# Down projection of a hybrid decoder layer: weight combinations moved to DVE, and the next pair of weight blocks emitted in two portions within the current pair

## The chip, the cores and the metric

One NeuronCore of a Trainium2 chip. A core has five engines with an instruction queue each: TensorE (PE in the profile, its weight loads PEld), VectorE (DVE), ScalarE (ACT), GpSimd (POOL) and SyncE (SP), which here only issues DMAs. Each queue is worked off in order; engines wait for each other by semaphores. The metric is the device time of one execution in microseconds; before the change the median of three runs is 1985.99 us (1985.06 to 1986.43).

## The reference

The kernel computes one layer of a hybrid decoder: a norm, one wide projection, four branches (gated recurrence, pooling, stick-breaking attention, short convolution), an output projection, and then an MLP with squared ReLU, for 1024 tokens and 1024 channels in float32. The change touches only the last product, `act` (1024 tokens x 4096) by `w_down` (4096 x 1024):

```python
    h2 = rmsnorm(x, norm2_g)
    act = jnp.square(jax.nn.relu(jnp.einsum('bld,df->blf', h2, w_up)))
    return x + jnp.einsum('blf,fd->bld', act, w_down)
...
    return rmsnorm(h[:, FRONT:], final_norm_g)
```

## The kernel before

All big products run on TensorE with float32 operands that are split into a high and a low part (`split`, lines 77 and 78: ACT casts the high part, DVE subtracts it from the source to get the low part). A product of two such operands is three matmuls: high by high, high by low, low by high.

**The down projection** takes the 4096 rows of `w_down` in 32 blocks of 128. The first four are multiplied plainly (line 1017 adds their products to `x1`, which is shown as `x`). The other 28 go through a Strassen scheme: two blocks of rows and the two halves of 512 columns make a 2 x 2 arrangement, whose product takes seven multiplications in place of eight, of combinations of the weight quarters and of the activations. The combinations of the activations were already formed in the up projection and lie in `sum_dram`. Those of the weights are formed by `down_w(u)` for u = 0 to 13.

`down_w(u)` loads two row blocks `w1` and `w2` (lines 1037 and 1038, tiles `raw`, two buffers in all, so one u at a time; for u = 1 tiles `lo`), forms four subtractions of 128x512 on POOL (lines 1046, 1048, 1049 and 1053, the first two into a tile `hi`), and splits five pieces into `h` and `l` (three of 512 columns, two of 1024). One call thus is 2 DMAs, 4 subtractions, 5 casts on ACT and 5 subtractions on DVE. The results lie in tiles `wb` or `wa`, by turns from pair to pair, four buffers of each name: two calls fill one name.

A **pair** `c` (0 to 6) uses the weights of u = 2c and 2c + 1, accumulated in PSUM. It has four **units** `m` (0 to 3), each for token blocks `m` and `m + 4`. A unit loads its activation combinations (`down_s`, line 1059, into `s_raw`, which has one buffer), splits them (`s_hi` by ACT, its low part in `wide` by DVE; then the remaining two blocks, named `s_late` or `lo` by turns) and does seven products of six matmuls each: 42 matmuls of 128x512, line 1081. The methods `one`, `two`, `three` and `four` of `Unit` hold the products; `two` and `four` of a unit are emitted after `one` and `three` of the next one. After each product DVE adds the bank to `x1` (lines 1088, 1092, 1096, 1100 and 1104) or writes the sum into the bank of product two (line 1086, tile `tr`), and one is copied by ACT (line 1098). A bank that DVE has yet to read is not written again, so the next product in the same bank waits for it: product six of a unit for line 1086.

**What sets the order.** The code is emitted as it stands in the loop over `c` and `m` at the end; a scheduler then fixes the order on each engine when the program is built, with emission order as priority, and hoists what is ready by its own estimate. Tiles come from rotating buffers: a tile's first write waits until the readers of its buffer's last use are done. In the loop before, both calls of `down_w` for a pair stand ahead of its four units:

```python
        for c in range(NU // 2):
            tw = [down_w(2 * c), down_w(2 * c + 1)]
...
            for m in range(4):
                unit = Unit(tw, c, m)
```

Of the kernel before, what the change touches and what calls it, by code (L numbers as in the profile page):

```python
# [47 lines left out]
def hybrid_trunk_kernel(ctx: ExitStack, tc: tile.TileContext, x_tok, metas, vecs, gains, w_in, w_br, w_pool,  # L48
                        w_o, w_up, w_dn, lvl_mask, out):
    nc = tc.nc  # L50
# [19 lines left out]
    def new(pl, shape, dt, tag, bufs=None):  # L70
        return pl.tile(shape, dt, tag=tag, name=nm(tag), **({} if bufs is None else {"bufs": bufs}))

    def split(hi, lo, src, eng=None, heng=None):
        if heng:
            heng.tensor_copy(hi, src)
        else:
            nc.scalar.copy(hi, src)  # L77
        (eng or nc.vector).tensor_sub(lo, src, hi.bitcast(F32))  # L78
# [118 lines left out]
    with ExitStack() as st:  # L197
# [192 lines left out]
        for i, (c0, n) in enumerate(FCH):  # L390
            last = i == len(FCH) - 1
# [524 lines left out]
    with ExitStack() as st:  # L916
# [12 lines left out]
        def pair_of(pl, tags, bufs, shape):  # L929
            return tuple(new(pl, shape, F32R, tag, bufs) for tag in tags)  # L930
# [102 lines left out]
        def down_w(u):  # L1033
            h, l = pair_of(dw, (("wb", "wb"), ("wa", "wa"))[u // 2 % 2], 4, [P, 7 * 512])
            f = FS + 2 * u
            w1, w2 = (new(wst, [P, D], F32, "lo" if u == 1 else "raw") for _ in range(2))
            nc.sync.dma_start(w1, w_dn[f])
            nc.sync.dma_start(w2, w_dn[f + 1])
            b11, b12, b21, b22 = w1[:, :512], w1[:, 512:], w2[:, :512], w2[:, 512:]
            ta = new(wst, [P, D], F32, "hi")  # L1040

            def put(c0, src):
                sl = (slice(None), slice(c0, c0 + src.shape[1]))
                split(h[sl], l[sl], src)

            nc.gpsimd.tensor_sub(ta[:, :512], b12, b11)
            put(0, b11)
            nc.gpsimd.tensor_sub(ta[:, 512:], b22, ta[:, :512])
            nc.gpsimd.tensor_sub(b12, b22, b12)
            put(512, w2)  # L1050
            put(1536, ta)
            put(2560, b12)
            nc.gpsimd.tensor_sub(b21, b21, ta[:, 512:])
            put(3072, b21)
            return h, l

# [80 lines left out]
        def final(b, eh):  # L1137
            es, fs = slice(eh * 512, (eh + 1) * 512), slice((1 - eh) * 512, (2 - eh) * 512)
            o = outs.pop()
            bias = new(small, [P, 1], F32, "bias")  # L1140
            nc.vector.tensor_scalar(bias, sum_sq(x1[:, b, fs], o[:, fs]), 4.0 / D, 4.0 * EPS, op0=ALU.mult, op1=ALU.add)
            nc.gpsimd.tensor_mul(x1[:, b, fs], x1[:, b, fs], fg[:, fs])
            y = rstd_of(sum_sq(x1[:, b, es], o[:, es]), D, bias)
            nc.scalar.mul(o[:, fs], x1[:, b, fs], y)
            nc.scalar.dma_start(out[b, :, fs], o[:, fs])
            nc.vector.scalar_tensor_tensor(o[:, es], x1[:, b, es], y, fg[:, es], op0=ALU.mult, op1=ALU.mult)
            nc.sync.dma_start(out[b, :, es], o[:, es])

        prev, last = None, NU // 2 - 1
        for c in range(NU // 2):  # L1150
            tw = [down_w(2 * c), down_w(2 * c + 1)]
            if c == last:
                fg = new(wst, [P, D], F32, "hi")
                nc.sync.dma_start(fg, gains[2])
                wide = [new(dw, [P, 7 * 512], F32, ("wa", "wb")[c % 2]) for _ in range(3)]
                outs = [t[:, i * D:(i + 1) * D] for t in wide for i in range(3)]
            for m in range(4):
                unit = Unit(tw, c, m)
                if c == last and m == 3:
                    unit.end(prev)  # L1160
                    break
                unit.one()
                if prev:
                    prev.two()
                unit.three()
                if c == last:
                    final(m, 1)
                if prev:
                    prev.four()
                    if c == last and m:  # L1170
                        final(prev.m + 4, 0)
                prev = unit


def _level_masks():
# [57 lines left out]
```

## Time and profile before

| | |
|---|---|
| median of three runs | 1985.99 us |
| profiled execution | 1990.17 us |
| its span in the profile | 1988.4 us |
| last matmul to the end of the span | about 8 us |
| down projection with Strassen, first line 1086 to the last matmul | 1698 to 1980 us |

The profile is of one execution. Its page begins with the busy time of each engine; a view by stretches gives the same for chosen windows, with the granted TensorE clock (1.00 is full speed), the mean share of the 16 DMA engines and the rate. A view of waits lists, for an engine, what it stood still for: total, number, longest. In a timeline row stand the start, the duration, the engine, the line, the operation, the output and input tiles, and in brackets the idle time just before it and what ended it. Starts in a full DVE queue lie closer together than the durations, since an instruction begins while the one ahead still drains. How the engines shared the last stretch of the stage:

```profile
1830.00:1880.00 50.00, 49.00 (x216) 40.27 (x215) 42.83 (x55) 20.56 (x27) 12.45 (x9) 1.00 0.42 149
1930.00:1988.00 58.00, 47.14 (x204) 38.07 (x204) 46.05 (x92) 28.70 (x62) 10.67 (x8) 0.97 0.34 120
```

After the bounds and the length of a window come the busy times of PE, PEld, DVE, ACT and POOL, each with its number of instructions.

### The profile page before, as it was taken

How to read it: one execution, taken by the hardware profiler on the slowest of the kernel's cores; microseconds unless marked ns; L12 is line 12 of the kernel's file. 1: busy time of each engine (PE TensorE's matmuls, PEld its weight loads, DVE VectorE, ACT ScalarE, POOL GpSimd, SP SyncE). 2: the span in 40 equal slices, each digit the busy share in tenths (PEclk: the TensorE clock that was granted, in tenths of full speed). 3: DMA queues.
4: the chain of work that ended last, by engine and by line, in shares of the span. 5: the costliest groups of instructions: out<-in, count | busy, mean ns of one | idle time of the engine just before them, and what ended most of it. 6: DMA issues, size and time to landing. Idle time of an engine off the chain costs nothing.

```text
span 1988.4 us, 25775 instructions
## 1 busy us (share of the span) xinstructions
PE 1934.6 (97%) x9974; PEld 1650.6 (83%) x9974; DVE 1294.7 (65%) x1783; ACT 844.2 (42%) x1452; POOL 329.9 (17%) x280
## 2 busy tenths in 40 slices
PE   9999999999998999999999999999999999999998
PEld 8889899988898888888887888788888887777876
DVE  6677877666767754344334567479555547888887
ACT  6556654233323433343333112255544544343435
POOL 1000001111100033333320000000323212222322
PEclk9999999999999999999999999999999999999999
DMA  3100111110102233333326554242454557343433
GB/s 130 42 33 22 42 34 49 54 43 33 33 32 80 74 151 125 148 107 128 118 105 235 187 187 161 79 147 88 140 170 138 154 164 256 127 143 140 152 131 137
DMA packets 112076, 224.61 MB, mean 113 GB/s; under 512 B 8129, under 2 KB 58817, under 8 KB 111954
## 3 DMA queue, kind: packets, MB, share of 16 engines
q1 hardware_dynamic: 56706, 175.22, 25.8%
q10 hardware_dynamic: 55248, 47.75, 7.1%
q8 instruction: 78, 1.28, 0.3%
q14 instruction: 44, 0.36, 0.1%
HBM read 157.40 MB, written 65.54 MB: 112 GB/s over the span
## 4 chain that ended last, share of the span: by engine, by line
PE 73%; DVE 11%; issue 9%; DMA 4%; ACT 3%; POOL 1%; POOLq 0%; ACTq 0%; DVEq 0%; SPq 0%
PE mm L704 18%; PE mm L104 9%; PE mm L103 9%; PE mm L102 9%; PE z L704 9%; PE tr L704 5%; PE mm L1081 2%; DMA s_raw<-sum_dram 2%; PE av L351 1%; PE z L571 1%; DVE wb L78 1%; DMA raw<-in_w_dn_dram 1%; DVE wa L78 1%; PE z L1081 1%; DVE keep L328 1%
## 5 line engine op out<-in xcount | busy, mean ns | idle before, releaser
L102 PE MATMUL mm<-h_hi,hi 128*128 128x384 f32 (+4 forms) x880 | 304.7, 347 | 0.4 <-ACT h_hi L77 0.4
L104 PE MATMUL mm<-h_hi,lo 128*128 128x384 f32 (+4 forms) x880 | 297.3, 338 | 5.8 <-DVE lo L78 5.8
L103 PE MATMUL mm<-h_lo,hi 128*128 128x384 f32 (+4 forms) x880 | 297.0, 338 | 0.5 <-DVE h_lo L78 0.4
L104 PEld LDWEIGHTS mm<-h_hi,lo 128*128 128x128 f32 x880 | 167.5, 190 | 14.2 <-DVE lo L78 6.2
L103 PEld LDWEIGHTS mm<-h_lo,hi 128*128 128x128 f32 x880 | 168.1, 191 | 7.2 <-DVE h_lo L78 1.3
L102 PEld LDWEIGHTS mm<-h_hi,hi 128*128 128x128 f32 x880 | 167.2, 190 | 6.9 <-ACT h_hi L77 0.9
L681 POOL TENSOR_TENSOR sf<-raw 128x512 f32<-128x512 f32 x30 | 40.9, 1363 | 772.0 <-DMA raw<-in_w_up_dram 448.8
L78 DVE TENSOR_TENSOR sl<-sf,sh 128x1024 fp32r<-128x1024 f32 x68 | 83.3, 1225 | 127.6 <-ACT sh L77 127.6
L78 DVE TENSOR_TENSOR lo<-raw,hi 128x1024 fp32r<-128x1024 f32 x76 | 96.3, 1267 | 52.6 <-ACT hi L77 52.4
L77 ACT CAST hi<-raw 128x1024 fp32r<-128x1024 f32 x76 | 79.9, 1053 | 79.7 <-PE mm L103 43.4
L704 PE MATMUL mm<-th,sh 128*128 128x512 f32 x272 | 105.9, 389 | 0.0
L704 PE MATMUL mm<-tl,sh 128*128 128x512 f32 x272 | 105.8, 389 | 0.0
L704 PE MATMUL mm<-th,sl 128*128 128x512 f32 x272 | 105.8, 389 | 0.0
L328 DVE TENSOR_TENSOR_SCAN keep<-keep 128x1040 f32<-128x1040 f32 (+3 forms) x64 | 88.9, 1389 | 25.7 <-ACT keep L321 18.9
L77 ACT CAST sh<-sf 128x1024 fp32r<-128x1024 f32 x68 | 71.5, 1052 | 80.2 <-PE z L704 41.7
L102 PE MATMUL mm<-b_hi,eh 128*128 128x512 f32 x256 | 99.6, 390 | 1.6 <-DVE mixed L873 1.6
L103 PE MATMUL mm<-b_lo,eh 128*128 128x512 f32 x256 | 100.1, 391 | 0.1
L104 PE MATMUL mm<-b_hi,el 128*128 128x512 f32 x256 | 99.6, 390 | 0.5 <-DVE el L78 0.5
L78 DVE TENSOR_TENSOR el<-raw,eh 128x512 fp32r<-128x512 f32 x34 | 36.6, 1076 | 61.8 <-ACT eh L77 61.8
L323 POOL TENSOR_SCALAR_AFFINE_SELECT keep<-keep 128x128 f32<-128x128 f32 x64 | 22.4, 350 | 302.2 <-ACT keep L321 262.1
L77 ACT CAST s_hi<-s_raw 128x1280 fp32r<-128x1280 f32 x28 | 35.4, 1265 | 85.2 <-DMA s_raw<-sum_dram 78.7
L77 ACT CAST at_h<-tr 128x384 fp32r<-128x384 f32 (+2 forms) x112 | 54.6, 496 | 36.5 <-PE tr L338 34.9
(439 smaller groups left out, 5019.8 us busy)
## 6 DMA issues: line engine op xcount, KB each, us to landing
raw<-in_w_in_dram SPq DMA_DIRECT2D x76, 512.0 KB, 3.6
s_raw<-sum_dram SPq DMA_DIRECT2D x28, 896.0 KB, 4.8
gate_dram<-go ACTq DMA_DIRECT2D x32, 512.0 KB, 2.6
go<-gate_dram SPq DMA_DIRECT2D x32, 512.0 KB, 3.9
raw<-in_w_up_dram SPq DMA_DIRECT2D x32, 512.0 KB, 3.7
raw<-in_w_dn_dram SPq DMA_DIRECT2D x29, 512.0 KB, 4.8
sum_dram<-go ACTq DMA_DIRECT2D x52, 256.0 KB, 4.6
sum_dram<-sums ACTq DMA_DIRECT2D x39, 256.0 KB, 4.6
```

What stands on the lines that cost most here:

```text
L77: nc.scalar.copy(hi, src)
L78: (eng or nc.vector).tensor_sub(lo, src, hi.bitcast(F32))
L102: nc.tensor.matmul(ps, lh, rh, start=first, stop=False)
L103: nc.tensor.matmul(ps, lh, rl, start=False, stop=False)
L104: nc.tensor.matmul(ps, ll, rh, start=False, stop=last)
L323: nc.gpsimd.affine_select(out=t[:, :P], in_=t[:, :P], compare_op=ALU.is_gt, fill=1.0, base=0, pattern=[[1, P]], channel_multiplier=-1)
L328: nc.vector.tensor_tensor_scan(t, t, t, 1.0, op0=ALU.mult, op1=ALU.min)
L351: nc.tensor.matmul(av[:, :w], pair.vv[e][:, b, :], a[:, b, :w], start=i == 0 and a is at[0], stop=i == len(order) - 1 and a is at[1])
L571: nc.tensor.matmul(ps[:, c * 64:(c + 1) * 64], xc, low, start=True, stop=True)
L681: eng.tensor_add(s12[:, 0], a21, a22)
L704: nc.tensor.matmul(ps, lhs[i][x][:, k, :], rhs[i][y][:, k, :], start=fresh and k == 0 and n == 0, stop=k == 3 and n == 2, skip_group_check ...
L1081: nc.tensor.matmul(ps, x, y[:, rs], start=fresh and k == 0 and n == 0, stop=k == 1 and n == 2, skip_group_check=not fresh)
```

## The change

The four subtractions of `down_w` are issued on DVE instead of POOL. And the two calls for the next pair are made inside the current pair: the first behind unit 1, the second behind unit 2; the two of pair 0 stay ahead of the loop. Lines behind the inserted one move by one to three.

```diff
-            nc.gpsimd.tensor_sub(ta[:, :512], b12, b11)
+            nc.vector.tensor_sub(ta[:, :512], b12, b11)
             put(0, b11)
-            nc.gpsimd.tensor_sub(ta[:, 512:], b22, ta[:, :512])
-            nc.gpsimd.tensor_sub(b12, b22, b12)
+            nc.vector.tensor_sub(ta[:, 512:], b22, ta[:, :512])
+            nc.vector.tensor_sub(b12, b22, b12)
             put(512, w2)
             put(1536, ta)
             put(2560, b12)
-            nc.gpsimd.tensor_sub(b21, b21, ta[:, 512:])
+            nc.vector.tensor_sub(b21, b21, ta[:, 512:])
             put(3072, b21)
             return h, l
...
         prev, last = None, NU // 2 - 1
+        coming = [down_w(0), down_w(1)]
         for c in range(NU // 2):
-            tw = [down_w(2 * c), down_w(2 * c + 1)]
+            tw, coming = coming, []
...
                     if c == last and m:
                         final(prev.m + 4, 0)
                 prev = unit
+                if c < last and m in (1, 2):
+                    coming.append(down_w(2 * c + 1 + m))
```

Three places show how the order moves. All are in pair 1; numbers behind a name tell buffers apart and differ between the two programs.

DVE, from the middle of unit 2 to the `wide` of unit 3. Before the change (`mm_14655`, `z_14656` and `tr_14657` are unit 2, `mm_14594` unit 1, `wide_14710` unit 3, `wb_14790` the second block of pair 2):

```order
L1086 TENSOR_TENSOR tr_14657<-mm_14655,x_2171_13933 128x512
L78 TENSOR_TENSOR wb_14790<-raw_14791,wb_14789 128x512
L1088 TENSOR_TENSOR x_2171_13933<-z_14656,x_2171_13933 128x512
L1092 TENSOR_TENSOR x_2171_13933<-mm_14594,x_2171_13933 128x512
L1096 TENSOR_TENSOR x_2171_13933<-mm_14655,x_2171_13933 128x512
L78 TENSOR_TENSOR wide_14710<-s_raw_14707,s_hi_14709 128x1280
```

With the change (`mm_14676` and `z_14677` are unit 2, `mm_14594` unit 1, `wide_14752` unit 3, `wb_14729` the second block of pair 2):

```order
L1096 TENSOR_TENSOR x_2171_13933<-mm_14676,x_2171_13933 128x512
L78 TENSOR_TENSOR wb_14729<-raw_14730,wb_14728 128x512
L1048 TENSOR_TENSOR hi_14734<-raw_14731,hi_14734 128x512
L1049 TENSOR_TENSOR raw_14730<-raw_14731,raw_14730 128x512
L1100 TENSOR_TENSOR x_2171_13933<-z_14677,x_2171_13933 128x512
L78 TENSOR_TENSOR wb_14729<-raw_14731,wb_14728 128x1024
L1104 TENSOR_TENSOR x_2171_13933<-mm_14594,x_2171_13933 128x512
L78 TENSOR_TENSOR wb_14729<-hi_14734,wb_14728 128x1024
L78 TENSOR_TENSOR wb_14729<-raw_14730,wb_14728 128x512
L1053 TENSOR_TENSOR raw_14731<-raw_14731,hi_14734 128x512
L78 TENSOR_TENSOR wide_14752<-s_raw_14749,s_hi_14751 128x1280
```

The second block's subtractions and splits now stand within unit 2, and unit 3's `wide` has moved behind lines 1100 and 1104. From the `wide` of unit 2 to that of unit 3 there are now 14 instructions of 128x512 and two of 128x1024 between them; before there were nine of 128x512. In pairs 2 to 5 this stretch reads the same with the change. The other stretches from one `wide` to the next have, with the change, six instructions of 128x512 (unit 0 to 1), eleven of 128x512 and two of 128x1024 (unit 1 to 2), and eleven of 128x512 (unit 3 to the next pair's unit 0).

TensorE, where it turns from unit 2 to unit 3. Before, with the last matmuls of unit 1's fourth product ahead:

```order
L1081 MATMUL mm_14594<-wa_14503,lo_14591 128x512
L1081 MATMUL mm_14716<-wa_14482,s_hi_14709 128x512
L1081 MATMUL mm_14716<-wa_14483,s_hi_14709 128x512
L1081 MATMUL mm_14716<-wa_14482,wide_14710 128x512
L1081 MATMUL mm_14716<-wa_14503,s_hi_14709 128x512
```

With the change; the last matmul of unit 1's fourth product, which releases line 1104 above, stands ahead of these, with four other rows between:

```order
L1081 MATMUL mm_14676<-wa_14443,s_late_14673 128x512
L1081 MATMUL mm_14758<-wa_14360,s_hi_14751 128x512
L1081 MATMUL mm_14758<-wa_14361,s_hi_14751 128x512
L1081 MATMUL z_14759<-wa_14360,s_hi_14751 128x512
L1081 MATMUL z_14759<-wa_14361,s_hi_14751 128x512
L1081 MATMUL mm_14676<-wa_14442,s_late_14673 128x512
L1081 MATMUL mm_14758<-wa_14360,wide_14752 128x512
```

Between the end of that fourth product and the first matmul that needs `wide` stand ten matmuls now, and two before: unit 2's late product and unit 3's high parts have been drawn in between. From the first matmul with one unit's `wide` to that of the next it is 38, 46, 42 and 42 matmuls with the change (unit 0 to 1, 1 to 2, 2 to 3, 3 to the next pair's unit 0), and 42 each before.

SP, the loads in pair 1 from unit 2 on, as a piece of the difference:

```order
-L1059 DMA s_raw_14646<-sum_dram 128x2x896
-L1037 DMA raw_14791<-in_w_dn_dram 128x1024
-L1059 DMA s_raw_14707<-sum_dram 128x2x896
-L1038 DMA raw_14792<-in_w_dn_dram 128x1024
+L1059 DMA s_raw_14667<-sum_dram 128x2x896
+L1037 DMA raw_14730<-in_w_dn_dram 128x1024
+L1038 DMA raw_14731<-in_w_dn_dram 128x1024
+L1059 DMA s_raw_14749<-sum_dram 128x2x896
+L1037 DMA raw_14934<-in_w_dn_dram 128x1024
+L1038 DMA raw_14935<-in_w_dn_dram 128x1024
 L1059 DMA s_raw_14810<-sum_dram 128x2x896
```

Both loads of the second block for pair 2 now stand ahead of unit 3's activations, and the first block for pair 3 is loaded ahead of pair 2's first unit instead of behind it. Each load of `raw` waits on SP's queue for its buffer, and the load of `s_raw` behind it with it.

## Prediction

> **What bounds the kernel now.** I read the page first, then the stretches of the down projection, then who makes TensorE wait there, then DVE and POOL around one such wait.
>
> ```profile
> PE 1934.6 (97%) x9974; PEld 1650.6 (83%) x9974; DVE 1294.7 (65%) x1783; ACT 844.2 (42%) x1452; POOL 329.9 (17%) x280
> core 0: us, PE busy (x) PEld busy (x) DVE busy (x) ACT busy (x) POOL busy (x), PEclk, DMA share, GB/s
> 1680.00:1730.00 50.00, 45.40 (x193) 35.37 (x192) 47.51 (x56) 20.12 (x26) 20.99 (x15) 1.00 0.39 127
> 1730.00:1780.00 50.00, 49.77 (x219) 40.63 (x218) 39.71 (x52) 18.78 (x25) 13.60 (x9) 1.00 0.42 143
> 1780.00:1830.00 50.00, 46.63 (x197) 37.47 (x196) 40.45 (x50) 22.11 (x30) 13.08 (x9) 0.97 0.39 135
> 1880.00:1930.00 50.00, 47.98 (x210) 38.88 (x208) 43.28 (x51) 21.16 (x30) 18.32 (x12) 1.00 0.44 151
> PE mm L1081 <- DVE tr L1086: 9.2, 7, 2.6
> PE mm L1081 <- DVE wide L78: 2.2, 3, 1.2
> ```
>
> TensorE is busy 97% of the span, and in this stage too it is the bound, less a few waits: the first stretch loses 4.6 us, the second 0.2. The second stretch gives its pace: 49.77 us over 219 matmuls, 0.227 us each, so a unit of 42 takes 9.54 us and a pair of four units 38.2. The waits are all on DVE: 9.2 us for the addition of line 1086, 2.2 for the low part `wide` of the activations. The table of waits is for the stage, 1670 to 1988.
>
> ```profile
> 1799.83 1.49 DVE L78 TENSOR_TENSOR wide<-s_raw,s_hi 128x1280 fp32r<-128x1280 f32 x1 [1.06 <-ACT s_hi L77]
> 1802.95 4.01 DVE L78 TENSOR_TENSOR wa<-raw,wa 128x512 fp32r<-128x512 f32 x2
> 1808.09 1.38 DVE L78 TENSOR_TENSOR wa<-hi,wa 128x1024 fp32r<-128x1024 f32 x1
> 1809.39 0.68 DVE L1086 TENSOR_TENSOR tr<-mm,x 128x512 f32<-128x512 f32 x1
> 1802.56 1.62 POOL L1048 TENSOR_TENSOR hi<-raw,hi 128x512 f32<-128x512 f32 x1
> 1804.13 1.75 POOL L1049 TENSOR_TENSOR raw<-raw,raw 128x512 f32<-128x512 f32 x1
> 1719.43 0.73 PE L1081 MATMUL mm<-wb,s_hi 128*128 128x512 f32 x2 [1.49 <-DVE tr L1086]
> ...
> 1810.13 0.73 PE L1081 MATMUL mm<-wb,s_hi 128*128 128x512 f32 x2 [2.57 <-DVE tr L1086]
> 1890.57 0.73 PE L1081 MATMUL mm<-wb,s_hi 128*128 128x512 f32 x2 [1.11 <-DVE tr L1086]
> 1931.70 0.74 PE L1081 MATMUL mm<-wa,s_hi 128*128 128x512 f32 x2 [2.62 <-DVE tr L1086]
> 1810.00:1815.00 5.00, 4.87 (x14) 3.87 (x15) 5.00 (x8) 0.95 (x3) 0.14 (x1) 0.66 0.51 189
> 1925.00:1935.00 10.00, 7.38 (x33) 5.77 (x32) 10.00 (x12) 4.22 (x6) 3.13 (x3) 1.00 0.27 92
> ```
>
> This is the mechanism. The second weight block of the next pair is prepared in the last unit of the current one. Two short splits, which alone take 0.68 each, cover 4.01 us, because beside them POOL works through its chain; line 1086 queues behind them and TensorE waits 2.57 us. The last two rows add the clock: after the wait of 2.57 it was granted 0.66 over 5 us, after the wait of 2.62 it stayed at 1.00. A half-clock stretch at 0.66 loses a third of 5 us, 1.7.
>
> What the pairs lose now follows from one instruction that each pair repeats, line 1086 of its first unit:
>
> ```profile
> 1736.71 0.69 DVE L1086 TENSOR_TENSOR tr<-mm,x 128x512 f32<-128x512 f32 x1
> 1938.83 0.70 DVE L1086 TENSOR_TENSOR tr<-mm,x 128x512 f32<-128x512 f32 x1 [0.67 <-PE mm L1081]
> ```
>
> From pair 1 to pair 6 that is 202.1 us for five pairs, 40.4 each, against 38.2: **2.2 us a pair, 11 us in all**, is what the change can win back there, wherever it comes from.
>
> **The change part by part.** POOL loses 14 blocks with four subtractions each, DVE gains them. Prices:
>
> ```profile
> L681 DVE TENSOR_TENSOR sf<-raw 128x512 f32<-128x512 f32 x4 | 2.7, 686 | 0.0
> L1046 POOL TENSOR_TENSOR hi<-raw 128x512 f32<-128x512 f32 x11 | 16.8, 1528 | 85.0 <-DMA raw<-in_w_dn_dram 85.0
> 1771.97 1.48 DVE L78 TENSOR_TENSOR wide<-s_raw,s_hi 128x1280 fp32r<-128x1280 f32 x1
> 1773.37 0.68 DVE L1100 TENSOR_TENSOR x<-z,x 128x512 f32<-128x512 f32 x1
> 1773.97 0.67 DVE L78 TENSOR_TENSOR lo<-s_raw,lo 128x512 fp32r<-128x512 f32 x1
> 1699.89 1.21 DVE L78 TENSOR_TENSOR wa<-raw,wa 128x1024 fp32r<-128x1024 f32 x1
> 1701.02 0.67 DVE L1096 TENSOR_TENSOR x<-mm,x 128x512 f32<-128x512 f32 x1
> ```
>
> DVE does the same operation on the same shape in 0.686 us in the up projection, where POOL needs 1.53 here. In a full queue starts follow each other at 0.60 (128x512), 1.13 (128x1024) and 1.40 (`wide`). A unit without weights is `wide` and seven of 0.60, 5.6 us; a weight block was three of 0.60 and two of 1.13, 4.06, and becomes 6.46. A pair's DVE work goes from 4 x 5.6 + 2 x 4.06 = 30.5 to 35.3 us, beside 38.2 of TensorE: it fits, if it is spread evenly. What DVE gets back from POOL is its stretching, and I take that as gone: all prices above are unstretched.
>
> The order shows that it is not even. Between `wide` of unit 2 and `wide` of unit 3, in each of pairs 1 to 5, DVE now has 14 instructions of 0.60, two of 1.13 and the second `wide`: 8.4 + 2.26 + 1.40 = **12.06 us, for 42 matmuls, 9.54 us**. Seven of them are a unit's own; the rest is nearly the whole second block and the last split of the first. A start made early cannot cover it: `wide` of unit 2 stands directly behind line 1104, which needs the last matmul of unit 0's fourth product, 10 matmuls (2.27 us) before TensorE needs that `wide`; 0.60 + 1.40 = 2.0 of them are used, so the slack is under 0.3. The lower bound comes from the same kind of place: line 1104 in front of unit 3's `wide` is released 10 matmuls before `wide` is needed, and line 1104, 1.13, 0.60, 0.60 and `wide` take 4.33: at least 2.1 us of waiting. The upper bound adds waits inside the 12.06: line 1048 needs the second raw block, whose load starts only when the former is split; if that lands a microsecond late the wait is 3.5. I take **2.5 us**, near the difference of 12.06 and 9.54, as the queue is full.
>
> What follows is the transfer of the activations, whose buffer is single:
>
> ```profile
> 1727.17 4.93 DMA s_raw<-sum_dram
> 1732.20 1.28 ACT s_hi L77
> 1733.50 1.49 DVE L78 TENSOR_TENSOR wide<-s_raw,s_hi 128x1280 fp32r<-128x1280 f32 x1 [2.13 <-ACT s_hi L77]
> 1774.67 6.46 DMA s_raw<-sum_dram
> ```
>
> From `wide` of unit 3, a split of weights and the late split (1.2), load (4.93, or 6.46 behind weight loads, as it now stands on SP's queue), 1.28 and 1.49: 8.9 to 10.5 us against 9.54. Nothing to 1.0 is lost; I take 0.3. SP's queue costs no more than that: the load ahead of this one waits for a split that DVE does just before the late split. From unit 0 to 1 and from 1 to 2 the chain takes 8.3, and DVE's 5.0 and 10.3 us meet 38 and 46 matmuls (8.6 and 10.4 us): nothing is lost. ACT keeps its casts and is busy 20 of 50 us: nothing. The losses without a listed wait stay: of the 11 us, the waits for line 1086 after 1736 (9.2 less the 1.49 of pair 0) and the clock's 1.7 explain 9.4, so about 0.3 a pair remain.
>
> So a pair loses 2.5 + 0.3 + 0.3 = 3.1 instead of 2.2, five pairs **4.5 us more**. Pair 0 has two crowded stretches, 9.1 and 12.06, and two of some 9.3 and 9.8 by transfer: 40.3 us, where now the `wide` of its first unit and that of pair 1 (1733.50) stand 38.6 apart: **1.7 more**.
>
> ```profile
> 1675.74 1.81 DVE L78 TENSOR_TENSOR wb<-raw,wb 128x512 fp32r<-128x512 f32 x1
> 1679.81 1.99 DVE L78 TENSOR_TENSOR wb<-hi,wb 128x1024 fp32r<-128x1024 f32 x1
> 1688.73 2.08 DVE L78 TENSOR_TENSOR wb<-hi,wb 128x1024 fp32r<-128x1024 f32 x1
> 1694.88 1.48 DVE L78 TENSOR_TENSOR wide<-s_raw,s_hi 128x1280 fp32r<-128x1280 f32 x1
> ```
>
> Ahead of pair 0 two blocks are prepared beside the last products of the first rows: eight subtractions, 4.8 us, join DVE's queue, and splits stretched like these three (by 1.1, 0.8 and 0.9 us) return to their price. With some six such splits this cancels; I take **0.5 more**, between 1 us gained and 1.5 lost. The clock, again in pairs 1 to 5: of two waits of 2.6 one was followed by a half-clock stretch. Five such waits give two or three; each costs 1.7 less the 0.3 that the transfer no longer costs, **3 more**. The last pair prepares no weights: nothing. Sum 9.7 on the profiled 1990.17 (1988.4 of span and 1.8 around it), 1999.9. The median is 4.2 below the profiled execution, so I put the 9.7 on 1985.99 and give 1996.
>
> [...]
>
> **The rivals.** *Faster: POOL's chain was the whole trouble.* Weights are ready a unit before they are needed, so no pair ends in a wait for line 1086, and the crowded stretch is absorbed. Then the 11 us of the five pairs shrink to 0.6 a pair, 3 us, and with pair 0 unchanged the time is 1978. For it: DVE's stretched rows, and a fuller TensorE in the second stretch above. Against it: the 12.06. It decides at 2.27 us: if DVE passes from line 1104 to the end of unit 3's `wide` within 10 matmuls, this wins. [...]
>
> *No change.* The wait stays at its floor, 2.1, without clock or slow transfers: 2.4 a pair, 1 more over five pairs, 1 in pair 0: 1988.
>
> *Much slower.* Each crowded stretch costs 3 us and halves the clock, and the transfer takes 6.46: 3 + 1.4 + 1.0 + 0.3 = 5.7 a pair, 17 more, with pair 0 2006. One such combination is in the trace, at 1810.
>
> *The change does not do what it says.* The order excludes it: the second block's last split now stands ahead of line 1086 of unit 3.
>
> **How the numbers follow.** Forecast (1992 to 2001) 0.55, much slower 0.15, no change 0.17, faster 0.13. 0.2% is 4 us, about what a measurement of this kernel can tell from no change. So slower 0.70, same 0.17, faster 0.13. The range leaves out most of the faster case and the far end of the slow one: 1984 to 2008.
>
> **What would show it.** Right: no POOL rows between 1700 and 1940; waits for line 1086 at pair starts under 0.5 us; a new wait of TensorE for `wide`, 2 to 3 us, once in pairs 1 to 5, in unit 3, with DVE gapless before it; DVE over 90% busy there. Line 1086 of first units some 41.5 apart. Wrong: waits for `wide` under 1 us, or DVE rows shorter than 0.60 apart, which would make the faster rival true; or line 1086 still late.

## The result and the profile after

| | before | after |
|---|---|---|
| median, four runs each, same chip | 1986.21 us (1985.06 to 1989.14) | **2005.24 us** (2003.11 to 2006.34) |
| profiled execution | 1990.17 us | 2005.66 us |
| its span | 1988.4 us | 2003.7 us |

The ratio is 1.0086, with a 95% interval of 1.0074 to 1.0098: slower by 19 us on the medians, by 15.3 us between the two profiled spans. The parts of the loss below are worked out against the latter.

The page of the changed kernel, its first line, and then the view by stretches of 50 us (bounds, length, then busy time of PE, PEld, DVE, ACT and POOL with numbers of instructions, granted clock, DMA):

```profile
PE 1942.9 (97%) x9974; PEld 1652.8 (82%) x9974; DVE 1308.6 (65%) x1839; ACT 842.3 (42%) x1452; POOL 249.1 (12%) x224
```

```profile
1730.00:1780.00 50.00, 47.66 (x198) 37.61 (x197) 41.85 (x59) 18.96 (x25) 0.00 (x0) 0.97 0.42 145
...
1880.00:1930.00 50.00, 47.37 (x198) 37.57 (x198) 43.20 (x59) 19.43 (x27) 0.00 (x0) 0.97 0.38 134
```

The first line hardly differs from that of before: still 97% on TensorE. The stretches tell more. POOL is at 0, DVE has seven and eight more instructions (52 and 51 before), and the stretch 1730 to 1780, which held 219 matmuls, holds 198. What TensorE waited for in 1670 to 2004 (total, number, longest), and then its longer waits (start, duration, in brackets the idle time ahead and what ended it):

```profile
PE mm L1081 <- DVE wide L78: 16.2, 7, 3.8
...
PE mm L1081 <- DVE tr L1086: 1.0, 2, 0.7
```

```profile
1697.88 0.50 PE L1081 MATMUL mm<-wb,wide 128*128 128x512 f32 x1 [3.83 <-DVE wide L78]
...
1770.33 0.50 PE L1081 MATMUL mm<-wa,wide 128*128 128x512 f32 x1 [2.20 <-DVE wide L78]
1813.60 0.50 PE L1081 MATMUL mm<-wb,wide 128*128 128x512 f32 x1 [2.63 <-DVE wide L78]
1855.81 0.50 PE L1081 MATMUL mm<-wa,wide 128*128 128x512 f32 x1 [1.18 <-DVE wide L78]
1899.10 0.50 PE L1081 MATMUL mm<-wb,wide 128*128 128x512 f32 x1 [2.63 <-DVE wide L78]
1942.43 0.50 PE L1081 MATMUL mm<-wa,wide 128*128 128x512 f32 x1 [2.63 <-DVE wide L78]
```

The wait for line 1086, 9.2 us before, has shrunk to 1.0; that for `wide` has grown from 2.2 to 16.2. Apart from the first it comes once in each of pairs 0 to 5, in unit 3 (the 1.12 of pair 0 is left out above). Why, DVE's rows of pair 2 show, from the `wide` of unit 2 to that of unit 3:

```profile
1799.44 1.48 DVE L78 TENSOR_TENSOR wide<-s_raw,s_hi 128x1280 fp32r<-128x1280 f32 x1
...
1807.38 0.69 DVE L1100 TENSOR_TENSOR x<-z,x 128x512 f32<-128x512 f32 x1 [0.23 <-PE z L1081]
...
1809.12 0.68 DVE L1104 TENSOR_TENSOR x<-mm,x 128x512 f32<-128x512 f32 x1
1809.72 1.21 DVE L78 TENSOR_TENSOR wa<-hi,wa 128x1024 fp32r<-128x1024 f32 x1
1810.85 0.68 DVE L78 TENSOR_TENSOR wa<-raw,wa 128x512 fp32r<-128x512 f32 x1
1811.46 0.68 DVE L1053 TENSOR_TENSOR raw<-raw,hi 128x512 f32<-128x512 f32 x1
1812.06 1.48 DVE L78 TENSOR_TENSOR wide<-s_raw,s_hi 128x1280 fp32r<-128x1280 f32 x1
```

DVE is never idle for more than a quarter of a microsecond, and still the second `wide` starts 12.62 us after the first, beside 42 matmuls that take 9.54. The weights are ready some 8 us before they are needed (the last split of this block starts at 1813.46, pair 3 begins at 1822.24); the activations now wait behind them.

Where the 15.3 us came from, by line 1086 of the first units. Each row below is the stretch from pair 1 to pair 6, five pairs, in the view by stretches; the first is of before, the second of after:

```profile
1736.71:1938.83 202.12, 193.79 (x839) 157.84 (x839) 170.29 (x211) 83.21 (x110) 56.54 (x37) 0.99 0.41 142
```

```profile
1739.66:1952.61 212.95, 200.15 (x837) 158.27 (x836) 180.47 (x246) 82.49 (x110) 0.00 (x0) 0.98 0.39 134
```

The five pairs took 10.8 us more: 212.95 less 202.12. TensorE's idle time, span less busy time, went from 8.3 to 12.8, which is 4.5; its busy time rose by 6.4, in part by the clock (below). The start cost 2.1 (line 1086 of the very first unit at 1700.15 instead of 1698.09), pair 0 cost 0.9 (39.51 instead of 38.62) and the last pair and the end 1.5 (51.09 instead of 49.57).

The clock shows when the view by stretches is laid on windows of 3.41 us around three of the waits (bounds, length, PE busy, granted clock, DMA):

```profile
1767.46:1770.87 3.41, 1.21 (x5) 1.00 0.40 135
1770.87:1774.28 3.41, 3.41 (x9) 0.50 0.66 231
...
1811.83:1815.24 3.41, 1.64 (x7) 1.00 0.51 163
1815.24:1818.65 3.41, 3.41 (x16) 1.00 0.92 334
...
1897.16:1900.57 3.41, 1.47 (x6) 1.00 0.44 154
1900.57:1903.98 3.41, 3.41 (x9) 0.50 0.77 264
```

After the waits that end at 1770.33 and 1899.10 TensorE ran at half clock for 3.41 us, 9 matmuls in place of 16; after that which ends at 1813.60, just as long, it did not, nor after that of 1942.43. A third half-clock window began at 1856.20. Before the change there was one in these pairs, at 1810.85. Each loses half of 3.41 us, 1.7.

### The profile page after: what moved, and what is told of

It is laid out like the page before. It is cut to its first block, busy times and chain, and to the rows that moved or that the text cites. A ratio compares the mean times of both kernels' runs of the same rounds, so it can differ in the third digit from the quotient of the medians.

```text
span 2003.7 us, 25730 instructions
## 1 busy us (share of the span) xinstructions
PE 1942.9 (97%) x9974; PEld 1652.8 (82%) x9974; DVE 1308.6 (65%) x1839; ACT 842.3 (42%) x1452; POOL 249.1 (12%) x224
## 4 chain that ended last, share of the span: by engine, by line
PE 79%; DVE 8%; issue 8%; ACT 2%; DMA 2%; POOL 1%; POOLq 0%; ACTq 0%; SPq 0%; DVEq 0%
PE mm L704 18%; PE mm L104 9%; PE mm L103 9%; PE mm L102 9%; PE z L704 9%; PE mm L1081 6%; PE tr L704 4%; PE z L1081 3%; PE tr L1081 2%; PE av L351 1%; PE z L571 1%; DVE keep L328 1%; DMA s_raw<-sum_dram 1%; PE tr L338 1%; DVE wide L78 1%
## 5 line engine op out<-in xcount | busy, mean ns | idle before, releaser
L78 DVE TENSOR_TENSOR at_l<-tr,at_h 128x384 fp32r<-128x384 f32 (+2 forms) x112 | 61.7, 568 | 12.4 <-ACT at_h L77 10.9
L321 ACT ACTIVATE keep<-z 128x272 f32<-128x272 f32 (+5 forms) x112 | 50.4, 457 | 29.2 <-PE z L319 28.2
```

The lines of the kernel that those rows point to most:

```text
L321: nc.scalar.activation(t, z, AF.Sigmoid, scale=-0.125)
```

## The experiments

Three theories stood against each other at first. **Crowding**: the loss comes from the second weight block standing in one stretch with a unit's own work. **Load**: DVE has too much to do, wherever it stands. **Early calls**: what harms is that the calls stand inside the pair at all, by their loads and by TensorE's other order. The first four kernels take the change apart and move its second part about.

**Only the subtractions on DVE**, the calls left where they were:

```diff
-            nc.gpsimd.tensor_sub(ta[:, :512], b12, b11)
+            nc.vector.tensor_sub(ta[:, :512], b12, b11)
...
-            nc.gpsimd.tensor_sub(b21, b21, ta[:, 512:])
+            nc.vector.tensor_sub(b21, b21, ta[:, 512:])
```

> The four subtractions on DVE, the calls where they were before (ahead of a pair's units). Three theories. Crowding: what costs time is that nearly the whole second block falls into one stretch from wide to wide (12.06 us of DVE work against 42 matmuls), with unit 3's wide behind line 1104. Here the order spreads the blocks over all four units: 8.5, 7.4, 10.9 and 8.6 us of DVE work against 39, 40, 47 and 42 matmuls (8.8, 9.1, 10.7, 9.5 us). So waits for wide of under 1 us, pairs of about 39.5 us instead of 42.6, and 1986 to 1992 us. Load: DVE has too much to do wherever it stands; its work is the same 35.3 us a pair, so the time is that of the changed kernel, 2003 to 2006. Early calls: the moved calls do the harm (loads ahead of the activations, TensorE's other order); without them 1982 to 1986.

Measured: 1984.38 us, ratio 0.9984 (0.9975 to 0.9993), a little faster than before the change. Of the three ranges it lies in that of the early calls, 1982 to 1986; crowding had put it at 1986 to 1992. Its stretch of five pairs, and the two longer of the four waits of TensorE from 1690 to the end:

```profile
1736.72:1932.23 195.51, 194.99 (x844) 156.48 (x843) 179.84 (x250) 82.87 (x110) 0.00 (x0) 1.00 0.44 146
```

```profile
PE mm L1081 <- DVE wide L78: 3.8, 1, 3.8
PE mm L1081 <- DVE x L1092: 1.8, 1, 1.8
...
```

DVE does as much as with the whole change (179.84 and 180.47 us), but the pairs take 39.1 us, not 42.6, and no listed wait is left in them: all four (the others are 0.7 and 0.2) lie at the start or in the last pair. DVE's load is not the cause. Most of the 0.9 us that a pair still takes above the pace of 38.2 are stops too short for the list; the part on the prediction comes back to them. And the wait for line 1086 did come from POOL's chain: in unit 3 of pairs 2 to 5 DVE does 12 instructions of 128x512 and two of 128x1024 between two `wide` in 10.9 us, where before it did ten and two in 12.1 to 12.6, without idle time in either.

**Only the calls moved**, the subtractions left on POOL:

```diff
+        coming = [down_w(0), down_w(1)]
...
-            tw = [down_w(2 * c), down_w(2 * c + 1)]
+            tw, coming = coming, []
...
+                if c < last and m in (1, 2):
+                    coming.append(down_w(2 * c + 1 + m))
```

> The subtractions back on POOL, the calls inside the current pair as in the change. Crowding: the fullest stretches have 9.7 and 10.3 us of DVE work against 44 and 45 matmuls (10.0 and 10.2 us), plus some 1.5 us a block by which POOL stretches DVE's splits; waits for wide of 1 us or so, pairs of 39.5 to 40.5, 1984 to 1991 us. Load: DVE is lighter by 4.8 us a pair, so as before or faster, 1978 to 1986. Early calls: as slow as the changed kernel, 2000 to 2006.

Measured: 1995.86 us, ratio 1.0042 (1.0028 to 1.0056), in none of the three ranges. Slower too, but by another wait. Of TensorE's waits from 1740 to 1950 the longest row, and POOL and ACT at one place in pair 3:

```profile
PE mm L1081 <- ACT s_hi L77: 12.1, 8, 2.2
```

```profile
1842.99 2.36 POOL L1049 TENSOR_TENSOR raw<-raw,raw 128x512 f32<-128x512 f32 x1
...
1845.31 2.27 POOL L1053 TENSOR_TENSOR raw<-raw,hi 128x512 f32<-128x512 f32 x1
...
1847.61 0.62 ACT L77 CAST wb<-raw 128x512 fp32r<-128x512 f32 x1 [1.12 <-POOL raw L1053]
1848.14 1.25 ACT L77 CAST s_hi<-s_raw 128x1280 fp32r<-128x1280 f32 x1
```

POOL's subtractions of line 1049, 1.54 us as a mean in these pairs before, are 1.88 as a mean here and 2.36 at this place. ACT's cast of a weight waits for the last of them, and `s_hi`, which needs only the activations, stands behind that cast in ACT's queue. So the move alone costs 0.42%, the subtractions alone gain 0.16%, and the two together cost 0.86%: the parts don't add up, because each decides in whose queue the activations wait.

**The calls behind the creation of units 1 and 3**, and then **behind that of units 1 and 2**; in both the subtractions are on DVE as in the change:

```diff
                 unit = Unit(tw, c, m)
+                if c < last and m in (1, 3):
+                    coming.append(down_w(2 * c + 2 + (1, 3).index(m)))
...
-                if c < last and m in (1, 2):
-                    coming.append(down_w(2 * c + 1 + m))
```

This is the difference to the changed kernel; the second kernel has `(1, 2)` in both places of the new lines.

> Subtractions on DVE; the next pair's calls behind the creation of unit 1 and of unit 3 instead of behind the work of units 1 and 2. The order gives 6.8, 10.9, 9.1 and 8.5 us of DVE work between wides against 42, 44, 40 and 42 matmuls, and wide stands behind line 1096 of the running unit, not behind line 1104. Crowding: no wait for wide over 1 us, pairs of 38.5 to 39.5, 1984 to 1990 us. Load: DVE's work per pair is unchanged, 2003 to 2006. Early calls: still inside the pair, so over 1995.

> Subtractions on DVE; the calls behind the creation of units 1 and 2, so half a unit earlier than in the change against the second block, but with wide of the coming unit ahead of it. The crowded stretch is as full as in the change, 12.07 us against 42 matmuls, yet wide stands behind line 1096 in it. Crowding by sum: the wait stays, but what a lighter stretch before saves can be carried over, so waits of 0.5 to 2 us a pair and 1990 to 1998. Only the tail behind line 1104 matters: waits vanish, 1984 to 1990. Load: 2003 to 2006.

Measured: 1984.57 us, ratio 0.9983 (0.9974 to 0.9992) for units 1 and 3; 2001.9 us, 1.0079 (1.0066 to 1.0092) for units 1 and 2. Five pairs of each, in this order, and the longest row of the latter's waits in 1740 to 1950:

```profile
1737.05:1933.52 196.47, 192.24 (x839) 156.41 (x838) 181.29 (x250) 83.59 (x110) 0.00 (x0) 1.00 0.46 146
```

```profile
1741.70:1953.56 211.86, 198.01 (x841) 158.74 (x840) 182.39 (x248) 84.48 (x110) 0.00 (x0) 0.98 0.41 132
```

```profile
PE mm L1081 <- ACT s_hi L77: 10.6, 9, 1.9
```

With the two blocks two units apart the pairs are as short as with no move, 39.3 us, though TensorE waits 0.5 to 1.6 us for `s_hi` once in each. So calls inside the pair do no harm by themselves: the theory of early calls, which expected over 1995 here, falls. With both blocks in neighbouring units the loss is back, though the crowded stretch lies a unit earlier and its `wide` is in time. The late split stands behind that `wide`, so the load into the single buffer `s_raw` starts late, and TensorE waits for the next unit's `s_hi`: in pair 2 the load starts at 1800.96 and lands at 1805.81, and TensorE goes on at 1807.21 after a wait of 1.76. No range held 2001.9: a smaller wait or none had been expected, not another one. The name of the wait changes with the order; the price nearly stays. Both kernels give DVE the same work (181.29 and 182.39 us busy), so load is excluded a second time.

**A lighter second block.** If the crowd is the cause, what it has too much must set the wait. Two kernels leave out some of the subtractions of the second block, everything else as in the change; in the first only the two last lines are put under the condition, in the second all four are, and the pieces that were split from `hi` are split from `raw` there:

```diff
-            nc.vector.tensor_sub(b12, b22, b12)
+            if u < 2 or u % 2 == 0: nc.vector.tensor_sub(b12, b22, b12)
...
-            nc.vector.tensor_sub(b21, b21, ta[:, 512:])
+            if u < 2 or u % 2 == 0: nc.vector.tensor_sub(b21, b21, ta[:, 512:])
```

> The changed kernel with two of the four subtractions of every second block (odd u from 3 on: lines 1049 and 1053) left out, so those weights are other ones. It sizes the crowded stretch. In the order, DVE's work from wide of unit 2 to wide of unit 3 is still 12.07 us, but 45 matmuls (10.21 us) instead of 42 stand beside it, and the tail behind line 1104 is 3.21 instead of 4.33. My theory (the wait is DVE's queue less the matmuls beside it): one wait for wide of 1.8 to 2.0 a pair in place of 2.63; then only 38 matmuls (8.62 us) stand against the transfer into the next pair, which took 10.16 in the changed kernel, so up to 1.5 comes back there. Line 1086 of first units 41.0 to 42.0 apart, time 1997 to 2003. Rival 1 (where the calls stand sets the loss, by transfers and loads, whatever DVE has to do): waits of 2.6 remain, time 2003 to 2007. Rival 2 (the half clock is most of it): waits under 2.2 are followed by no half clock, and the time falls by 5 or more, below 2000.

> The changed kernel with all four subtractions of every second block (odd u from 3 on) left out, so those weights are other ones. In the order the crowded stretch is then 10.87 us of DVE beside 45 or 47 matmuls (10.2 to 10.7 us). My theory: the wait for wide in unit 3 falls to 0.2 to 0.7, the transfer into the next pair costs 0.3 to 1.5 as 38 matmuls (8.62 us) stand against it; line 1086 of first units 39.3 to 40.5 apart, time 1988 to 1995. Rival 1 (where the calls stand sets the loss): waits of 2.6 remain, 2002 to 2006. Rival 2 (DVE's load as a whole): 2.4 us less work in a pair of 42.6, of which DVE is busy 86%, changes little, 2000 to 2004.

Measured: 1990.86 us, ratio 1.001 (1.0002 to 1.0019), with two left out; 1988.21 us, 0.9998 (0.999 to 1.0007), with four. For each, the two `wide` of a crowded stretch, a wait at such a place and the five pairs; first the kernel with two left out, then that with four:

```profile
1795.75 1.48 DVE L78 TENSOR_TENSOR wide<-s_raw,s_hi 128x1280 fp32r<-128x1280 f32 x1
1808.20 1.49 DVE L78 TENSOR_TENSOR wide<-s_raw,s_hi 128x1280 fp32r<-128x1280 f32 x1
```

```profile
1849.93 0.50 PE L1081 MATMUL mm<-wa,wide 128*128 128x512 f32 x1 [1.51 <-DVE wide L78]
```

```profile
1739.30:1940.11 200.81, 193.45 (x841) 156.57 (x840) 174.61 (x238) 81.14 (x110) 0.00 (x0) 1.00 0.41 142
```

```profile
1793.38 1.48 DVE L78 TENSOR_TENSOR wide<-s_raw,s_hi 128x1280 fp32r<-128x1280 f32 x1
1804.64 1.48 DVE L78 TENSOR_TENSOR wide<-s_raw,s_hi 128x1280 fp32r<-128x1280 f32 x1
```

```profile
1806.18 0.50 PE L1081 MATMUL mm<-wb,wide 128*128 128x512 f32 x1 [0.52 <-DVE wide L78]
```

```profile
1736.23:1934.12 197.89, 193.62 (x842) 156.77 (x841) 168.71 (x227) 81.46 (x110) 0.00 (x0) 1.00 0.42 144
```

Less the matmuls beside it, the stretch is 12.62 - 9.54 = 3.1 us too long in the changed kernel, 12.45 - 10.21 = 2.2 with two left out and 11.26 - 10.21 = 1.1 with four; the wait is 2.63, 1.51 and 0.52. It follows the excess, 0.5 to 0.7 below it. With two left out DVE's work in the stretch stays the same; it is the three matmuls more beside it (45, not 42) that lower the excess. With four left out wait, distance and time came out as my theory expected. With two left out the wait stood in the expected place, but it was shorter than the 1.8 to 2.0 expected, and the time was to lie between 1997 and 2003 and fell to 1990.9. That is the outcome named there for the half clock. Against the changed kernel the five pairs lost 12.1 us: 5.4 of idle time (12.8 to 7.4) and 6.7 of busy time, of which three half-clock windows are 5.1. Here a wait of 1.5 cost its length, and one of 2.6 could cost 1.7 more. The transfer into the next pair, feared at up to 1.5, cost nothing: from the `wide` at 1808.20 to the next it took 8.65, not 10.16.

**The second block's subtractions on POOL**, the rest as in the change:

```diff
-            nc.vector.tensor_sub(ta[:, :512], b12, b11)
+            (nc.gpsimd if u > 1 and u % 2 else nc.vector).tensor_sub(ta[:, :512], b12, b11)
```

The other three lines are changed in the same way.

> The changed kernel, but the subtractions of every second block (odd u from 3 on) are issued on POOL; nothing is left out. DVE's order is that of the kernel without them: 10.87 us in the crowded stretch. If only DVE's own instructions count: 1988 to 1995, as without them. If POOL's chain beside DVE stretches the splits by 1 to 2 us a block as it does before the change, and delays the casts behind it: waits of 1.5 to 2.6 for wide or s_hi in unit 3, 1995 to 2003.

Measured: 2004.1 us, ratio 1.0082 (1.0068 to 1.0096), no better than the change and outside both ranges. POOL, ACT and TensorE at one of the waits:

```profile
1763.82 2.26 POOL L1053 TENSOR_TENSOR raw<-raw,hi 128x512 f32<-128x512 f32 x1
...
1766.11 0.62 ACT L77 CAST wb<-raw 128x512 fp32r<-128x512 f32 x1 [1.60 <-POOL raw L1053]
1766.64 1.25 ACT L77 CAST s_hi<-s_raw 128x1280 fp32r<-128x1280 f32 x1
...
1767.94 0.73 PE L1081 MATMUL mm<-wa,s_hi 128*128 128x512 f32 x2 [2.56 <-ACT s_hi L77]
```

The same as with the calls moved alone: taking four instructions off DVE's queue puts the activations behind POOL, in ACT's queue. The waits named by the second expectation came, 1.5 to 2.6 there, 2.2 to 2.9 here; four of the five long ones are for `s_hi`, the longest is for `wide`.

**The first two blocks on POOL.** The change also slowed the start. Three kernels leave u = 0 and 1 on POOL: the change, the kernel with only the subtractions moved, and the one with the calls in units 1 and 3.

```diff
-            nc.vector.tensor_sub(ta[:, :512], b12, b11)
+            (nc.gpsimd if u < 2 else nc.vector).tensor_sub(ta[:, :512], b12, b11)
```

Again the other three lines likewise.

> The changed kernel, but the subtractions of the two blocks ahead of pair 0 (u = 0 and 1) stay on POOL, as before the change. My reading: the 2.06 us by which line 1086 of the first unit came later are DVE's eight extra subtractions; the first wait for wide falls from 3.83 to 1.2 to 2.2, and the half clock behind it may go: 1.5 to 3.5 us less, 2001.5 to 2004. Rival (the start's loss is made up later, as unit 0 of pair 0 waits anyway): no difference, 2004.5 to 2006.

> The subtractions on DVE, the calls where they were before the change, and the two blocks ahead of pair 0 (u = 0 and 1) left on POOL. In the changed kernel the same exception moved line 1086 of the first unit from 1700.15 to 1694.24, but pair 0 then took 1.2 us longer and the later pairs 2.0. If what is won at the start stays won: line 1086 of the first unit at about 1694.5, pairs 1 to 5 at 39.1 each as without the exception, 3 to 5 us less than the kernel with all subtractions on DVE: 1979 to 1982, ratio to before 0.9955 to 0.9975. Rival (pair 0's units wait for the same loads and splits afterwards, and all of it is given back): 1983 to 1986, ratio 0.998 to 1.0.

> The subtractions on DVE, the calls for the next pair behind the creation of units 1 and 3, and the two blocks ahead of pair 0 left on POOL. If what is won at the start stays won: 3 to 5 us less than without that exception, 1979 to 1982. Rival (given back in pair 0): 1983 to 1986. In both no stretch from one wide to the next holds more DVE work than 10.9 us for 44 to 47 matmuls, so no wait of 1.8 us or more and no half clock is expected from the second pair to the sixth; a half clock there would speak against the reading that the clock follows such waits.

Measured: the change with this exception 2003.26 us, ratio 1.0074 (1.0061 to 1.0086); the subtractions alone with it 1982.94 us, 0.9971 (0.996 to 0.9982); units 1 and 3 with it **1980.49 us, 0.9964 (0.9951 to 0.9976)**, the fastest of all. Line 1086 of the first unit starts at 1694.24 in the first and at 1692.81 in the third of these. The five pairs of the third:

```profile
1731.62:1927.81 196.19, 192.42 (x840) 156.60 (x839) 181.51 (x249) 83.82 (x110) 0.00 (x0) 1.00 0.45 145
```

In the change with this exception the first unit comes 5.9 us earlier (1694.24 instead of 1700.15), the first wait for `wide` is 0.91 instead of 3.83, and no half clock follows it. That is mostly given back: pair 0 takes 1.2 us more and the five pairs 2.0, as a fourth half-clock window falls into them. The time, 2003.26, lies in the range expected, but the 2 us won are not clear of noise: the intervals of the two kernels overlap. With the blocks spread out 4 us of what is won stay on the medians (1984.57 to 1980.49), as expected. With the subtractions alone 1.4 stay (1984.38 to 1982.94), below the expected 3 to 5, and that difference is not clear of noise: in the profile the first unit comes 4.3 us earlier, and the five pairs take 197.7 instead of 195.5. As expected, neither of these two kernels had a half clock from the second pair to the sixth.

## Why the prediction was right, and where its sizes were off

The direction, the mechanism and the place were right: slower, by a wait for `wide` in unit 3 behind a crowded DVE, in all of pairs 1 to 5. The gain on line 1086 came as foreseen and was paid back elsewhere. The size was too small: 9.7 us forecast against 15.3 between the profiles, 10 against 19 on the medians. The time lies above the 1992 to 2001 of the forecast itself, within the wider range. Term by term:

- **Crowded stretch, 12.06 us and a wait of 2.5.** Measured in pair 2: 12.62 and 2.63. The 0.6 are two short stops of DVE ahead of lines 1086 and 1100, which wait for products (0.2 and 0.3 us), and starts slightly wider than 0.60. The transfer behind it, 10.16 from one `wide` to the next, lies within the 8.9 to 10.5 given; TensorE waits 0.22 for `s_hi` there, and 0.3 a pair had been forecast. (In the three pairs with a half clock it took 11.4, with TensorE itself slower.) The five pairs' idle time rose by 4.5 us. That this is the 4.5 of the forecast is chance: the latter was to hold the stops outside the list, too, and takes off the one half-clock window of before.
- **Clock, 3 us.** "Two or three" half-clock windows were forecast; there were three, 5.1 us, where before there was one.
- **Losses without a listed wait, 0.3 a pair, "stay".** This step failed; it is the largest miss within the pairs. Of the 6.4 us by which TensorE's busy time rose, two more half-clock windows are 3.4; the other 3.0 are such losses. They come in pairs without a half clock too: 169 matmuls are listed as 39.34 us busy in pair 2, and as 38.76 with two subtractions left out (below). In the five pairs of the changed kernel there are 17 places, outside the half-clock windows, where TensorE stops too briefly for the list: a matmul starts 0.03 to 0.3 us behind the pace of 0.227, and mostly the one after it 0.11 behind again. Together they take 3.0 us; before the change there was one such place, of 0.1. The first row below is one of them: `wide` of unit 2 has only just ended (1799.44, 1.48 long), so the slack that the prediction put at under 0.3 was gone. The second is the same matmul with two subtractions left out, where there is no such stop in pair 2. They do not come from the crowded stretch alone: the kernel with only the subtractions on DVE has 18, 3.8 us.

```profile
1800.98 0.50 PE L1081 MATMUL mm<-wb,wide 128*128 128x512 f32 x1
```

```profile
1797.67 0.39 PE L1081 MATMUL mm<-wb,wide 128*128 128x512 f32 x1
```

```profile
1782.91:1825.10 42.19, 39.34 (x169) 31.13 (x168) 36.56 (x50) 16.42 (x22) 0.00 (x0) 1.00 0.40 137
```

```profile
1779.49:1819.67 40.18, 38.76 (x169) 31.32 (x168) 35.28 (x48) 16.28 (x22) 0.00 (x0) 1.00 0.40 144
```

- **Ahead of pair 0, 0.5.** It was 2.1, above the bound of 1.5. The step that failed is "with some six such splits this cancels": five splits there were stretched by 4.4 us in all and did get their price back, against the 4.8 added. But the first `wide` still started 1.5 us later (1696.34, not 1694.88). Two additions of line 1017, which stood behind it before (1696.29 and 1696.88), now stand ahead of it, 1.2 us; DVE's queue begins 0.35 later there; and one split has moved behind it, 0.6 less. TensorE waited 3.83 us for it instead of 1.19, and a half clock followed at 1699.19, which the step had left out.
- **Pair 0, 1.7.** It was 0.9.
- **The last pair, nothing.** It was 1.5: its listed waits rose from 1.3 to 2.5, 0.9 of it by the wait for line 1092, which the subtractions alone show too (1.8 above). Why the end is ordered less well there wasn't followed up.
- **A reading.** The row "4.01 us, x2" is not two short splits: the trace has one of 128x512, 1.77 long, and one of 128x1024, 2.32 long, which alone take 0.68 and 1.21. The stretching was real, about 2.2 us in that place instead of the 2.7 that the text suggests; no term of the sum used it.
- **The base.** The sum was put on the median. The profiled execution of before lay 4.0 us above its median, that of after 0.4, so 3.5 of the 19 us were never in the comparison of the profiles. Added to the profiled 1990.17, as worked out, the forecast would have read 1999.9.

Of the signs named, these came: no POOL work between 1700 and 1940, line 1086 on time at the starts of pairs (a weak sign: before the change too its longer waits from 1736 on stood at the ends, in unit 3), a new wait of 2 to 3 us for `wide` (2.20, 2.63, 1.18, 2.63 and 2.63; that of 1.18 followed one of 1.17 for `s_hi` in the same unit). Line 1086 of first units stood 42.6 apart, not 41.5. DVE was busy throughout the crowded stretch, as expected, and 85% over a pair (36.1 of 42.6 us).

Of the rivals, "POOL's chain was the whole trouble" was right about POOL: without the move its removal wins 5.5 us of span between the profiles, 0.16% in the ratio. It was wrong about the crowded stretch, which came with the move. "Much slower", at a chance of 0.15, gave nearly the time that came, 2006, by the same crowd with the half clock in every pair. That it met the time is luck: the clock came in three pairs of five, and the five pairs lost 10.8 us where that rival had 17. The start, the last pair and the base made up the rest.

## What to carry to other kernels

Preparing the next tile's operands earlier helps only if each stretch between two deadlines has room for them: count an engine's work between two instructions that TensorE waits for, not over the whole loop, and spread the blocks until no stretch exceeds its matmuls by much (here 12.62 us of DVE beside 9.54 us of matmuls cost a wait of 2.63, and the same work spread out left no wait above 1.6 in the pairs). Moving work to another engine and moving it in time can cost together where one of them alone gains (ratio 1.0086 with both here, 0.9984 with the engine alone), since both change which queue the urgent operand waits in; test them apart. Look at the clock behind each wait: here waits of up to 1.5 us cost their length, and some of 1.8 and more cost 1.7 again.

## What the runs showed of the hardware

The half-clock windows lie on a fixed grid. In the changed kernel they begin at 1770.87, 1856.20 and 1900.57: 85.33 and 44.37 us apart, 25 and 13 times 3.413, and each is itself 3.413 long in the trace. So it is not the length of a wait that decides in these runs, but how much of it falls into one cell of the grid, a stretch of 3.413 us. From 1690 to 1970, over the twelve profiles, 24 cells ran at half clock. Ahead of 22 of them lay a cell with 1.8 us or more of listed waiting; ahead of one, the cell at 1852.79 of the changed kernel, 1.6; and one was the second of two in a row. Of the other cells of the ten profiles in which such cells occur, nearly 800, none had more than 1.77 of waiting in the cell ahead; in the remaining two the longest wait was 1.83. So the border lies near 1.8 here, but it is not sharp. The waits of 2.63 that cost nothing in the clock were cut in two by a cell's edge: the one that ended at 1813.60 began at 1810.97, and the edge at 1811.83 left 0.86 on one side and 1.77 on the other. The same holds for the pair of waits in the prediction: that of 2.57 lay in the cell before 1810.85, and the one of 2.62 was cut at 1930.31. Of the profile before the change, first the two cells of the former wait, then those of the latter:

```profile
1807.44:1810.85 3.41, 0.84 (x4) 1.00 0.00 0
1810.85:1814.26 3.41, 3.41 (x10) 0.50 0.52 184
...
1926.90:1930.31 3.41, 2.18 (x10) 1.00 0.75 260
1930.31:1933.73 3.42, 2.03 (x9) 1.00 0.00 0
```

A part of a cell was enough: 2.57 us of waiting ahead of 1810.85, and in the changed kernel 2.20 ahead of 1770.87 and 1.94 ahead of 1900.57. With 1.8 as the border, a wait of 2.63 at a random place in the grid halves the clock unless the edge leaves less than 1.8 on both sides, (1.8 - 0.83) / 3.41 or 28% of the places: an estimate from these numbers, 3.6 of five, where the prediction took two or three and three came.
